# One running sum of the exponentials per attention unit, shared by VectorE and GpSimd

## The chip, the cores and the metric

The kernel runs on one core of a Trainium2 chip. The core has five engines with an instruction queue each: TensorE (PE, matmuls; its weight loads are shown apart as PEld), VectorE (DVE), ScalarE (ACT), GpSimd (POOL) and SyncE (SP), which only starts DMAs here. An engine takes its instructions strictly in the order of its queue; an instruction that waits holds everything behind it on the same engine. Engines are tied together by semaphores alone. The metric is the device time of one execution in microseconds.

## The reference

A trunk of two layers over 256 context and 1024 latent tokens of width 1024: a state-space mixer, then an attention mixer with 16 query heads and 4 key/value heads of 64, and a final norm. All is fp32. What matters here is the attention of the second layer, for the latent tokens only, with keys and values of all 1280 tokens:

```python
def attend(q, k, v):
    ...
    s = jnp.einsum('bqgrd,bkgd->bgrqk', q, k).astype(F32) * (A_HEADDIM ** -0.5)
    p = jax.nn.softmax(s, axis=-1).astype(v.dtype)
    o = jnp.einsum('bgrqk,bkgd->bqgrd', p, v)
...
o_lat = (ol * jax.nn.silu(gl)) @ out_w
...
h_lat = h_lat + gt[:, None] * o_lat
return rmsnorm(h_lat, final_norm_w)
```

## The kernel before

The first three quarters of the time go to the first layer and the projections of the second; the change leaves their instructions and order as they are. The attention and the output projection follow from 1475.6 us on.

**Units.** Attention is done in 16 units (`units`, `NU`): one unit is a pair of heads and 512 queries. A unit has ten key tiles of 128 keys (`kt`, `NT`). For each key tile, PE computes the scores of both heads into a PSUM buffer of 128 × 1024 (tag `sc`, three buffers; L1729, four matmuls a head: three for the split of fp32 into two parts, and one that subtracts the queries' maxima through a row of the query tile), ACT takes the exponential into an SBUF tile `P` of 128 × 1024 (L1734, six buffers), and PE multiplies it with the values into `ot` (L1745). The columns of `P` are queries, its partitions keys, so the softmax divisors are a sum over the ten tiles and then over the partitions. The first is done by adds of whole tiles into `acc` (L1710, L1754), the second by a matmul with ones (`divisors`, L1767, into PSUM tag `dn`).

**Divisors.** `keep` (L1771, ACT) copies `dn` into `rb`; `compact` (L1780) gathers one row of each head by DMA into `rv`, a 128 × 8 tile; DVE takes the reciprocals (L1787); two DMAs write them out (L1788) and spread them over the partitions again (L1784, into `rb`). Then `rb` is multiplied with the gate `sg` (L1790, POOL) and with the unit's output `ob` into `at` (L1791, DVE).

**Maxima.** The maxima of a unit's scores are computed ahead of it, from matmuls of their own with the queries as weights (`maxima`, L1528): ten tiles into `sc` buffers too, each reduced by DVE straight from PSUM (L1675), then one small reduction (L1543), a transpose on PE (L1684), a copy (L1687) and a DMA that puts them in the query tile (L1547). Units 0 and 1 have theirs from an earlier stage, so 14 units' maxima lie in this one.

**Rounds.** A unit is five rounds of two key tiles. In round r = 5u + j of unit u, PE's order is: first maxima tile of a later unit, scores of key tiles 2j and 2j + 1, second maxima tile, values of the round before. The maxima of unit u' are those of rounds 5u' − 8 to 5u' − 4. The divisors of unit u stand behind the values in round 5u + 6, the transpose of maxima at the end of a round whose number is 2 modulo 5. PE's order is given by numbers (`pe`, `turns`); the other engines' order comes from `Plan.order()`, a small planner that runs through the operations by rank, duration and dependencies, as written in each `plan.op`. What it gives is fixed in the program: the engines don't choose.

**PSUM.** With three `sc` buffers taken in turn by first maxima, two scores and second maxima, the second maxima of a round use the buffer that the first used, and can start only when DVE has reduced those.

**The two sums.** `SUM_POOL` gives key tiles 0, 1, 3, 5, 7 to POOL and the others to DVE. Each engine keeps a sum of its own (`acc` in two tags, one buffer each): POOL makes 0 + 1, then adds 3, 5, 7; DVE makes 2 + 4, then adds 6, 8, 9; a last DVE add (L1754) joins the two. POOL also does L1790 and, in eight units, the low part of a weight of the output projection (L1830, `wol`).

**Projection.** `project_out` runs over eight tiles of 128 tokens; the first four need only units 0 to 7. The high and low part of the first (`first`, L1857 and L1861) are made early, among the units. The rest stands behind the last unit.

Of the kernel before, what the change touches and what calls it, by code (L numbers as in the profile page):

```python
# [12 lines left out]
OP = mybir.AluOpType  # L13
# [16 lines left out]
SUM_POOL = (0, 1, 3, 5, 7)  # L30
WE = 4
SC_ACT, LO_POOL = (1, 4, 7), (1, 3, 5, 7)
# [113 lines left out]
def emit(tc, A, out):  # L146
# [1477 lines left out]
    with ExitStack() as st:  # L1624
# [10 lines left out]
        plan = Plan({"q": 3, "sc": 3, "ot": 1, "dn": 1, "P": NP, "accP": 1, "accV": 1, "mx": 2, "rb": 2, "sg": 2, "ob": 2, "wr": 4, "first": 2, "rv": 2})  # L1635
# [7 lines left out]
        held, shifts, brought, finished, last_scores, turns = {}, {}, {}, {}, [], []  # L1643

# [15 lines left out]
        def maxima(u):  # L1660
# [3 lines left out]
            for i in range(10):  # L1664
# [13 lines left out]
                rs.append(plan.op("DVE", reduce, [a], R + 10 * i - 60, 1.22, takes=[] if i else [hm], uses=[hs, hm]))  # L1678
            a = plan.op("DVE", lambda: largest(t["m"][1], t["m"][0]), rs, R + 30, .25, uses=[hm])
# [10 lines left out]
        def unit(u):  # L1690
# [3 lines left out]
            ho, hg, ha = plan.hold("ot"), plan.hold("sg"), {e: plan.hold("acc" + e[0] if e == "POOL" else "accV") for e in ("POOL", "DVE")}  # L1694
            sums = {"POOL": [], "DVE": []}
# [5 lines left out]
            def add_up(*tiles, e, rank):  # L1701

                if len(tiles) == 1:
                    return
                E, (k0, e0, h0), (kt, e1, h1), two = G if e == "POOL" else V, tiles[0], tiles[-1], len(tiles) == 2

                def add():
                    if two:
                        t[e] = S4.tile([128, 1024], FT, tag="acc" + e, bufs=1, name="acc")
                    E.tensor_tensor(t[e], t["P", k0] if two else t[e], t["P", kt], op=OP.add)  # L1710
# [5 lines left out]
            pv = None  # L1716
            for j in range(5):
# [31 lines left out]
                for i, kt in enumerate(kts):  # L1749
                    e = "POOL" if kt in SUM_POOL else "DVE"  # L1750
                    sums[e].append((kt, es[i], hp[i]))
                    add_up(*sums[e], e=e, rank=R + 10 * kt + 10)
            hd, hb, he = plan.hold("dn"), plan.hold("rb"), plan.hold("ob")
            a = plan.op("DVE", lambda: V.tensor_tensor(t["DVE"], t["DVE"], t["POOL"], op=OP.add), [t["aPOOL"], t["aDVE"]], R + 110, 1.3,  # L1754
                        uses=list(ha.values()))

# [7 lines left out]
            def divisors():  # L1764
                t["d"] = psum("dn", [128, 512])
                for h in range(2):
                    T.matmul(t["d"][h * 64:(h + 1) * 64], ones[:, 0:64], t["DVE"][:, h * 512:(h + 1) * 512], start=True, stop=True)  # L1767
# [5 lines left out]
            a = pe(5 * u + (6.6 if u < NU - 1 else 5.6), divisors, [a], R, .87, takes=[hd], uses=[ha["DVE"]], table="cols")  # L1773
# [8 lines left out]
            def spread():  # L1782
                for h, r in enumerate(HALF):
# [6 lines left out]
            a = plan.op("POOL", lambda: G.tensor_tensor(t["r"], t["r"], t["g"], op=OP.mult), [a, g], R + 90, 1.4, uses=[hb, hg])  # L1790
            finished[u] = plan.op("DVE", lambda: V.tensor_tensor(at[b][:, p], t["b"], t["r"], op=OP.mult), [a, ev], R + 90, .66,  # L1791
                                  uses=[hb, he])
# [43 lines left out]
        def table(i, src):  # L1836
            def bring():
                tabs[i] = S4.tile([128, 1024], FT, tag="acc" + ("POOL", "DVE")[i], bufs=1, name="tab")
                Q.dma_start(tabs[i], rows(src, 128))
# [144 lines left out]
```

## Time and profile before

| | us |
|---|---|
| runs shown: lowest, median, highest | 1970.56, 1971.6, 1972.78 |
| profiled execution: time, span of the core | 1970.99, 1969.2 |
| attention, first scores to the end of the last round with maxima | 1475.6 to 1829.1 |
| last two units and output projection on PE | 1829.1 to 1954.9 |
| after PE's last matmul | 1954.9 to 1969.2 |

Over the whole span PE is busy for 97%, DVE for 73%, ACT for 57%, POOL for 57%. These shares are averages over very different stages, so they are read by stretches here. A row of the timeline gives the start, the duration, the engine, the line of the kernel, what the instruction writes and reads, its shapes and a count; square brackets tell how long the engine stood idle before it and what released it. Matmuls overlap, so PE's busy time also holds small waits between them. The granted clock of PE is 1.00 all through the attention.

### The profile page before, as it was taken

How to read it: one execution, taken by the hardware profiler on the slowest of the kernel's cores; microseconds unless marked ns; L12 is line 12 of the kernel's file. 1: busy time of each engine (PE TensorE's matmuls, PEld its weight loads, DVE VectorE, ACT ScalarE, POOL GpSimd, SP SyncE). 2: the span in 40 equal slices, each digit the busy share in tenths (PEclk: the TensorE clock that was granted, in tenths of full speed). 3: DMA queues.
4: the chain of work that ended last, by engine and by line, in shares of the span. 5: the costliest groups of instructions: out<-in, count | busy, mean ns of one | idle time of the engine just before them, and what ended most of it. 6: DMA issues, size and time to landing. Idle time of an engine off the chain costs nothing.

```text
span 1969.2 us, 30433 instructions
## 1 busy us (share of the span) xinstructions
PE 1906.2 (97%) x10552; PEld 1448.0 (74%) x10552; DVE 1440.6 (73%) x1784; ACT 1115.2 (57%) x2055; POOL 1113.6 (57%) x940
## 2 busy tenths in 40 slices
PE   8999999999999999999999999999999999999997
PEld 2788788888888888888788878877774444444485
DVE  4677996979788786766446897877657888888533
ACT  4557767677867686777544775533224444444511
POOL 2305775668576766756388787753444444544422
PEclk9999999999999999999999999999999999999998
DMA  8125645444644546265585785533232111111123
GB/s 303 33 62 148 173 132 159 129 152 134 174 142 125 154 135 193 83 188 151 192 271 183 245 261 174 165 118 97 86 112 71 44 50 54 54 55 39 51 79 107
DMA packets 167614, 259.82 MB, mean 132 GB/s; under 512 B 24906, under 2 KB 60618, under 8 KB 167460
## 3 DMA queue, kind: packets, MB, share of 16 engines
q1 hardware_dynamic: 166308, 256.04, 42.7%
q8 instruction: 83, 1.36, 0.3%
q10 hardware_dynamic: 1152, 1.84, 0.2%
q14 instruction: 71, 0.58, 0.1%
HBM read 214.97 MB, written 42.69 MB: 131 GB/s over the span
## 4 chain that ended last, share of the span: by engine, by line
PE 69%; DVE 11%; POOL 2%; issue 2%; DMA 1%; ACT 1%; SPq 0%; DVEq 0%; POOLq 0%; ACTq 0%
PE ob L169 7%; PE pj L169 7%; PE pj L171 7%; PE ob L171 7%; PE pj L170 7%; PE ob L170 7%; PE ot L1745 6%; PE sc L1729 6%; PE yo L903 3%; DVE acc L1710 2%; PE sc L1528 2%; PE st L784 2%; DVE acc L711 2%; PE yd L861 2%; DVE mx L1675 1%
## 5 line engine op out<-in xcount | busy, mean ns | idle before, releaser
L169 PE MATMUL pj<-inh,whi 128*128 128x512 f32 (+1 forms) x1152 | 441.5, 383 | 0.5 <-DVE dv L519 0.5
L171 PE MATMUL pj<-inh,wlo 128*128 128x512 f32 (+1 forms) x1152 | 409.5, 355 | 1.2 <-POOL wlo L668 1.2
L170 PE MATMUL pj<-inl,whi 128*128 128x512 f32 (+1 forms) x1152 | 408.4, 355 | 0.0
L171 PEld LDWEIGHTS pj<-inh,wlo 128*128 128x128 f32 x1152 | 217.0, 188 | 33.3 <-POOL wlo L668 1.4
L711 DVE SCALAR_TENSOR_TENSOR acc<-ub,convw,acc 128x1282 f32<-128x1282 f32 x128 | 230.2, 1799 | 14.5 <-ACT acc L708 11.4
L169 PEld LDWEIGHTS pj<-inh,whi 128*128 128x128 f32 x1152 | 218.1, 189 | 28.5 <-issue 2.2
L1734 ACT ACTIVATE P<-sc 128x1024 f32<-128x1024 f32 x160 | 156.2, 1023 | 143.5 <-PE sc L1729 143.5
L170 PEld LDWEIGHTS pj<-inl,whi 128*128 128x128 f32 x1152 | 218.2, 189 | 25.5
L826 ACT ACTIVATE W<-lab,u_t 128x128 f32<-128x128 f32 x640 | 202.5, 391 | 50.0 <-POOL lab L820 24.4
L1675 DVE TENSOR_REDUCE mx<-sc 128x2 f32<-128x1024 f32 (+1 forms) x140 | 170.4, 1217 | 62.1 <-PE sc L1528 62.1
L820 POOL TENSOR_SCALAR_AFFINE_SELECT lab<-lab 128x512 f32<-128x512 f32 x160 | 146.7, 922 | 119.1 <-DMA lab<-la_d 110.0
L779 POOL TENSOR_TENSOR xw<-xst,te_t 128x256 f32<-128x256 f32 x144 | 147.4, 1039 | 23.7 <-PE st L784 12.0
L1745 PE MATMUL ot<-P,vv 128*64 128x512 f32 x640 | 155.0, 605 | 0.0
L1710 POOL TENSOR_TENSOR acc<-acc,P 128x1024 f32<-128x1024 f32 x48 | 115.5, 2406 | 54.9 <-ACT P L1734 53.7
L668 POOL TENSOR_TENSOR wlo<-wraw,whi 128x512 fp32r<-128x512 f32 x48 | 71.1, 1481 | 125.1 <-ACT whi L665 109.7
L1729 PE MATMUL sc<-q,kh 64*128 64x512 f32 x640 | 127.2, 393 | 0.2 <-ACT P L1734 0.2
L171 PE MATMUL ob<-whi,yl 128*128 128x512 f32 x288 | 113.9, 395 | 1.9 <-DVE yl L1127 1.3
L169 PE MATMUL ob<-whi,yh 128*128 128x512 f32 x288 | 114.6, 398 | 0.0
L170 PE MATMUL ob<-wlo,yh 128*128 128x512 f32 x288 | 113.7, 395 | 0.0
L968 DVE SCALAR_TENSOR_TENSOR macc<-mraw,cc,macc 128x512 f32<-128x512 f32 x98 | 107.8, 1122 | 2.9 <-DMA mraw<-in_mod_w 2.9
L798 POOL TENSOR_TENSOR tm<-PV,dec_t 128x512 f32<-128x512 f32 x64 | 89.5, 1398 | 35.2 <-DVE PV L802 33.6
L839 DVE TENSOR_TENSOR W<-W 128x512 f32<-128x512 f32 x80 | 73.9, 924 | 39.8 <-ACT W L826 38.6
(302 smaller groups left out, 4401.5 us busy)
## 6 DMA issues: line engine op xcount, KB each, us to landing
lab<-la_d SPq DMA_DIRECT2D x160, 256.0 KB
wraw<-in_w_in SPq DMA_DIRECT2D x96, 256.0 KB
workvv<-in_m_out_w SPq DMA_DIRECT2D x94, 256.0 KB
mraw<-in_mod_w SPq DMA_DIRECT2D x64, 256.0 KB
es<-e_d SPq DMA_DIRECT2D x128, 128.0 KB
wraw<-in_wqkv SPq DMA_DIRECT2D x48, 256.0 KB
q_d<-qs SPq DMA_DIRECT2D x64, 128.0 KB
q<-q_d SPq DMA_DIRECT2D x32, 256.0 KB
```

The lines of the kernel that those rows point to most:

```text
L169: T.matmul(o, lh, rh, start=first, stop=False)
L170: T.matmul(o, lh, rl, start=False, stop=False)
L171: T.matmul(o, ll, rh, start=False, stop=last)
L711: V.scalar_tensor_tensor(t["a"], ub[i % 2][:, k:k + CW], convw[:, ct, k:k + 1], t["a"], op0=OP.mult, op1=OP.add)
L779: G.tensor_tensor(t[d], s["xst"][:, c], te_t[:, d, c, h4][:, :, None].to_broadcast([128, 4, 64]), op=OP.mult)
L820: G.affine_select(t["l", d], t["l", d], [[0, 4], [sgn, 128]], OP.is_ge, NEVER, base=0, channel_multiplier=-sgn)
L826: S.activation(t["w", d][:, h], t["l", d][:, h], AF.Exp, bias=u_t[:, d, c, 4 * g + h:4 * g + h + 1])
L1675: V.tensor_reduce(max_place(t["m"][0], i), o, AX.X, OP.max)
L1710: E.tensor_tensor(t[e], t["P", k0] if two else t[e], t["P", kt], op=OP.add)
L1729: T.matmul(o[:, h], (first_row[r] if n == 3 else (kh, kl, kh)[n][r, kv, k]), x[(0, 0, 1, 2)[n]][r], start=(n == 0), stop=(n == 3))
L1734: S.activation(t["P", kt], flat(t["s", kt]), AF.Exp)
L1745: T.matmul(t["o"][h * 64:(h + 1) * 64], vv[:, kt, kv], t["P", kt][:, h * 512:(h + 1) * 512], start=(kt == 0), stop=(kt == NT - 1))
```

## The change

One sum per unit takes the place of two. DVE makes 0 + 1 and adds tiles 3, 5 and 7 (`SUM_DVE`); POOL adds tiles 2, 4, 6, 8 and 9 to the same `acc`. Each add waits for the one before it, so the two engines take turns, but for 8 and 9, which are both POOL's. There is no joining add. `acc` is one tag with two buffers, so the next unit's sum can begin before this one's is used.

The DVE adds get fixed places: `reduced[r]` is the reduction of the first maxima of round r, and `behind(r)` makes an operation wait for it in the plan. The first add of unit u stands behind that of round 5u + 1, tile kt's behind that of round 5u + 1 + kt // 2. The product with the gate moves from POOL to DVE, behind the first reduction of round 5u + 10, and so do the low parts of the early weights (one unit earlier than before). POOL's add of tile 9 waits for the product of the unit before (`finished[u - 1]` in the plan, and a dependency of the instruction itself on `scaled_by[u - 1]`). The two tables of the output projection use `acc`'s buffers as before, held as such.

```diff
-SUM_POOL = (0, 1, 3, 5, 7)
+SUM_DVE = (3, 5, 7)
...
-        plan = Plan({"q": 3, "sc": 3, "ot": 1, "dn": 1, "P": NP, "accP": 1, "accV": 1, "mx": 2, "rb": 2, "sg": 2, "ob": 2, "wr": 4, "first": 2, "rv": 2})
+        plan = Plan({"q": 3, "sc": 3, "ot": 1, "dn": 1, "P": NP, "acc": 2, "mx": 2, "rb": 2, "sg": 2, "ob": 2, "wr": 4, "first": 2, "rv": 2})
...
+        reduced, scaled_by = {}, {}
+
+        def behind(r):
+            return [reduced[r]] if r in reduced else []
...
+                if i % 2 == 0:
+                    reduced[5 * u - 8 + i // 2] = rs[-1]
...
-                t["a" + e] = plan.op(e, add, [e1, e0 if two else t["a" + e]], rank, 2.45 if e == "POOL" else 1.3,
-                                     takes=[ha[e]] if two else [], uses=[ha[e], h1] + ([h0] if two else []))
+            def add_first():
+                t["a"] = S4.tile([128, 1024], FT, tag="acc", bufs=2, name="acc")
+                V.tensor_tensor(t["a"], t["P", 0], t["P", 1], op=OP.add)
+
+            def add(kt):
+                x = (V if kt in SUM_DVE else G).tensor_tensor(t["a"], t["a"], t["P", kt], op=OP.add)
+                if kt == NT - 1 and u:
+                    tc.add_manual_dep(x.ins, scaled_by[u - 1].ins.name, mybir.DependencyInfo(mybir.DependencyClass.Sync, mybir.DependencyReason.DATA),
+                                      reason="sums")
+
+            def add_up():
+                last = plan.op("DVE", add_first, exps[0:2] + behind(5 * u + 1), R + 10, 1.25, takes=[ha], uses=[ha, *hps[0:2]])
+                for kt in range(2, NT):
+                    dve = kt in SUM_DVE
+                    last = plan.op("DVE" if dve else "POOL", lambda kt=kt: add(kt),
+                                   [last, exps[kt]] + (behind(5 * u + 1 + kt // 2) if dve else [finished[u - 1]] if kt == NT - 1 and u else []),
+                                   R + 10 * kt + 10, 1.25 if dve else 2.42, uses=[ha, hps[kt]])
+                return last
...
-            a = plan.op("DVE", lambda: V.tensor_tensor(t["DVE"], t["DVE"], t["POOL"], op=OP.add), [t["aPOOL"], t["aDVE"]], R + 110, 1.3,
-                        uses=list(ha.values()))
...
-            a = plan.op("POOL", lambda: G.tensor_tensor(t["r"], t["r"], t["g"], op=OP.mult), [a, g], R + 90, 1.4, uses=[hb, hg])
-            finished[u] = plan.op("DVE", lambda: V.tensor_tensor(at[b][:, p], t["b"], t["r"], op=OP.mult), [a, ev], R + 90, .66,
-                                  uses=[hb, he])
+            def scaled():
+                scaled_by[u] = V.tensor_tensor(at[b][:, p], t["b"], t["r"], op=OP.mult)
+
+            a = plan.op("DVE", lambda: V.tensor_tensor(t["r"], t["r"], t["g"], op=OP.mult), [a, g] + behind(5 * u + 10), R + 90, .66, uses=[hb, hg])
+            finished[u] = plan.op("DVE", scaled, [a, ev], R + 90, .66, uses=[hb, he])
...
-                R = 100 * (4 + 2 * kt + h) + 50 if kt < WE else 100 * NU + 10 * kt + 5 * h
+                R = 100 * (3 + 2 * kt + h) + 85 if kt < WE else 100 * NU + 10 * kt + 5 * h
...
-                after = last_scores if kt >= WE else [finished[3 + 2 * kt + h]]
+                after = last_scores if kt >= WE else [finished[2 + 2 * kt + h]]
+                early_slot = behind(5 * (5 + 2 * kt + h)) if kt < WE else []
...
-                wparts[kt, h] = plan.op("POOL" if kt < WE else "DVE", lambda t=t, f=part, E=G if kt < WE else V:
-                                        E.tensor_tensor(f(1), t["w"], f(0).bitcast(FT), op=OP.subtract), [a], R,
-                                        1.44 if kt < WE else .8, uses=[raw])
+                wparts[kt, h] = plan.op("DVE", lambda t=t, f=part: V.tensor_tensor(f(1), t["w"], f(0).bitcast(FT), op=OP.subtract), [a] + early_slot,
+                                        R, .7, uses=[raw])
```

DVE's queue of before, where unit 5's own sum begins (`acc_16466`, rounds 27 to 29; `mx` are reductions of maxima, `rv` the reciprocals of the unit before):

```order
L1675 TENSOR_REDUCE mx_16439<-sc_16424 128x2
L1675 TENSOR_REDUCE mx_16439<-sc_16456 128x2
L1710 TENSOR_TENSOR acc_16466<-P_16400,P_16454 128x1024
L1787 RECIPROCAL rv_16451<-rv_16451 128x8
L1675 TENSOR_REDUCE mx_16439<-sc_16471 128x2
L1675 TENSOR_REDUCE mx_16439<-sc_16500 128x2
L1710 TENSOR_TENSOR acc_16466<-acc_16466,P_16497 128x1024
L1675 TENSOR_REDUCE mx_16439<-sc_16512 128x2x2
L1675 TENSOR_REDUCE mx_16439<-sc_16542 128x2
L1710 TENSOR_TENSOR acc_16466<-acc_16466,P_16538 128x1024
L1675 TENSOR_REDUCE mx_16439<-sc_16553 128x2
L1710 TENSOR_TENSOR acc_16466<-acc_16466,P_16549 128x1024
```

The first two adds stand behind a round's second reduction, the later ones here and there; the joining add comes four rows further on.

DVE's queue of the changed kernel, rounds 25 to 27 (`acc_16401` is unit 5's sum; `rb` and `at` are unit 3's; the first row is the first reduction of round 25):

```order
L1680 TENSOR_REDUCE mx_16218<-sc_16332 128x2
L1838 TENSOR_TENSOR wol_15286<-wr_15316,woh_15285 128x512
L1799 TENSOR_TENSOR rb_16216<-rb_16216,sg_15937 128x512
L1797 TENSOR_TENSOR at0_15296<-ob_16170,rb_16216 128x512
L1680 TENSOR_REDUCE mx_16218<-sc_16357 128x2
L1680 TENSOR_REDUCE mx_16218<-sc_16373 128x2
L1709 TENSOR_TENSOR acc_16401<-P_16354,P_16367 128x1024
L1680 TENSOR_REDUCE mx_16218<-sc_16403 128x2x2
L1543 TENSOR_REDUCE nm0_10263<-mx_16218 128x8
L1680 TENSOR_REDUCE mx_16435<-sc_16421 128x2
L1712 TENSOR_TENSOR acc_16401<-acc_16401,P_16413 128x1024
L1680 TENSOR_REDUCE mx_16435<-sc_16453 128x2
```

Every add now stands between a round's first and second reduction; one round in five has the three products there instead.

POOL's queue of before, units 4 to 5 (`acc_16417` is POOL's sum of unit 5):

```order
L1790 TENSOR_TENSOR rb_16218<-rb_16218,sg_15932 128x512
L1830 TENSOR_TENSOR wol_15286<-wr_15316,woh_15285 128x512
L1710 TENSOR_TENSOR acc_16417<-P_16358,P_16370 128x1024
L1710 TENSOR_TENSOR acc_16417<-acc_16417,P_16415 128x1024
L1710 TENSOR_TENSOR acc_16417<-acc_16417,P_16463 128x1024
L1710 TENSOR_TENSOR acc_16417<-acc_16417,P_16507 128x1024
L1790 TENSOR_TENSOR rb_16436<-rb_16436,sg_16146 128x512
```

And POOL's queue of the changed kernel, the last add of unit 4 and those of unit 5:

```order
L1712 TENSOR_TENSOR acc_16184<-acc_16184,P_16328 128x1024
L1712 TENSOR_TENSOR acc_16401<-acc_16401,P_16399 128x1024
L1712 TENSOR_TENSOR acc_16401<-acc_16401,P_16450 128x1024
L1712 TENSOR_TENSOR acc_16401<-acc_16401,P_16492 128x1024
L1712 TENSOR_TENSOR acc_16401<-acc_16401,P_16533 128x1024
L1712 TENSOR_TENSOR acc_16401<-acc_16401,P_16545 128x1024
```

POOL has nothing but adds of the one sum, five a unit, each of tiles that DVE has handed on. PE's order is the same in both kernels up to the last unit; there the last divisors stand behind 24 matmuls of the projection's first tile, of which 12 stood behind them before.

More of the change, by code (lines that the diff above doesn't have):

```diff
@@ L1693, in unit @@
             x, q = qs3[u % 3], held[u]
-            ho, hg, ha = plan.hold("ot"), plan.hold("sg"), {e: plan.hold("acc" + e[0] if e == "POOL" else "accV") for e in ("POOL", "DVE")}
-            sums = {"POOL": [], "DVE": []}
+            ho, hg, ha = plan.hold("ot"), plan.hold("sg"), plan.hold("acc")
             def gate():
@@ L1837, in bring @@
             def bring():
-                tabs[i] = S4.tile([128, 1024], FT, tag="acc" + ("POOL", "DVE")[i], bufs=1, name="tab")
+                tabs[i] = S4.tile([128, 1024], FT, tag="acc", bufs=2, name="tab")
                 Q.dma_start(tabs[i], rows(src, 128))
-            return plan.op("SP", bring, [], 100 * NU + 200, takes=[plan.hold(("accP", "accV")[i])], move=1.75)
+            return plan.op("SP", bring, [], 100 * NU + 200, takes=[tab_holds[i]], move=1.75)
+        tab_holds = [plan.hold("acc") for _ in range(2)]
         in_tabs = [table(0, m_d[0, 3072:4096]), table(1, A["final_norm_w"])]
```

26 lines of the change are left out of this document (8 added, 18 removed).

## The prediction

> **What bounds the kernel now.** I read the busy time by stretches first, then the waits in the stretch that the change touches, then the chain that ended last there, then the timeline of one unit. The change leaves everything before 1475.6 us as it was, so only what follows counts. Stretches: length, then busy us of PE, PEld, DVE, ACT, POOL, granted clock, DMA share, GB/s.
>
> ```profile
> 1481.80:1829.10 347.30, 328.29 (x2089) 169.21 (x2087) 293.84 (x251) 161.34 (x189) 160.91 (x78) 1.00 0.16 48
> 1829.10:1954.90 125.80, 125.69 (x595) 88.34 (x593) 49.01 (x69) 39.56 (x63) 42.51 (x31) 1.00 0.25 80
> ```
>
> The first row is rounds 2 to 71 of attention, those with maxima of a later unit beside the scores. The second is the last two units (no maxima) and the output projection: PE is busy for 125.69 of 125.80 us, so nothing is to be had there. In the first, PE has 19.0 us without work and DVE is busy for 85%. Waits there (engine, line, who released it: total us, times, longest):
>
> ```profile
> PEld sc L1528 <- DVE mx L1675: 30.5, 29, 1.9
> PE sc L1528 <- DVE mx L1675: 18.9, 16, 1.5
> ```
>
> So PE waits, about twice in each of 14 units, for a reduction on DVE to free a PSUM buffer. What makes the reduction late shows in one unit on the timeline (start, us, engine, line, tiles, count, idle time before it):
>
> ```profile
> 1600.15 0.51 PE L1528 MATMUL sc<-kh,q 64*128 64x512 f32 x2
> ...
> 1605.41 0.50 PE L1528 MATMUL sc<-kh,q 64*128 64x512 f32 x2
> ...
> 1608.96 2.38 POOL L1710 TENSOR_TENSOR acc<-acc,P 128x1024 f32<-128x1024 f32 x1 [0.92 <-ACT P L1734]
> 1609.16 3.25 DVE L1710 TENSOR_TENSOR acc<-P 128x1024 f32<-128x1024 f32 x1
> ...
> 1610.00 0.50 PE L1528 MATMUL sc<-kh,q 64*128 64x512 f32 x2
> ...
> 1612.45 1.17 DVE L1675 TENSOR_REDUCE mx<-sc 128x2 f32<-128x1024 f32 x1
> ...
> 1613.67 0.50 PE L1528 MATMUL sc<-kh,q 64*128 64x512 f32 x2 [1.34 <-DVE mx L1675]
> 1613.93 2.36 POOL L1710 TENSOR_TENSOR acc<-acc,P 128x1024 f32<-128x1024 f32 x1 [2.59 <-ACT P L1734]
> ...
> 1615.36 2.01 DVE L1710 TENSOR_TENSOR acc<-acc,P 128x1024 f32<-128x1024 f32 x1
> ...
> 1615.97 0.50 PE L1528 MATMUL sc<-kh,q 64*128 64x256 f32 x4
> ...
> 1618.56 0.50 PE L1528 MATMUL sc<-kh,q 64*128 64x512 f32 x2 [0.23 <-DVE mx L1675]
> ...
> 1620.25 1.22 DVE L1710 TENSOR_TENSOR acc<-acc,P 128x1024 f32<-128x1024 f32 x1
> 1620.86 0.50 PE L1528 MATMUL sc<-kh,q 64*128 64x512 f32 x2
> ...
> 1621.41 1.23 DVE L1675 TENSOR_REDUCE mx<-sc 128x2 f32<-128x1024 f32 x1
> ...
> 1622.55 1.22 DVE L1710 TENSOR_TENSOR acc<-acc,P 128x1024 f32<-128x1024 f32 x1
> ...
> 1623.06 0.40 PE L1528 MATMUL sc<-kh,q 64*128 64x512 f32 x2
> ...
> 1623.68 0.69 DVE L1791 TENSOR_TENSOR at<-ob,rb 128x512 f32<-128x512 f32 x1
> ...
> 1624.28 1.22 DVE L1675 TENSOR_REDUCE mx<-sc 128x2 f32<-128x1024 f32 x1
> 1624.97 1.28 POOL L1830 TENSOR_TENSOR wol<-wr,woh 128x512 fp32r<-128x512 f32 x1 [6.10 <-ACT woh L1828]
> 1625.26 0.19 PEld L1528 LDWEIGHTS sc<-kh,q 64*128 64x128 f32 x2 [0.81 <-ACT woh L1828]
> ```
>
> The same add of 1024 columns takes 1.22 us at 1620.25 and 1622.55, with POOL silent, but 3.25 at 1609.16, where a POOL add had started 0.20 earlier. That POOL add ends at 1611.34, the DVE add at 1612.41, 1.07 later; the add of 2.01 us at 1615.36 ends 1.08 after its POOL neighbour (1613.93 + 2.36 = 1616.29). So a DVE add that meets a running POOL add stands until that is done and then runs. The reduction behind it starts at 1612.45, and PE, which in an undisturbed round issues its second maxima 2.20 us in (1620.86 to 1623.06), gets to them 3.67 us into the round that began at 1610.00. Rounds, from one first maxima matmul to the next: 1600.15 to 1605.41, 5.26 (with the divisors); to 1610.00, 4.59 (with the transpose); to 1615.97, **5.97**; to 1620.86, **4.89**; to 1625.26, 4.40. The last is a round without a wait. A unit of such rounds is 5.26 + 4.59 + 3 × 4.40 = **23.05 us**. What it takes now, from the chain that ended last (start, us, what), divisors of unit 0 and of unit 12:
>
> ```profile
> 1505.58 0.86 PE dn L1767 x4
> ...
> 1803.52 0.86 PE dn L1767 x4
> ...
> 1833.31 2.04 PE sc L1729 x16
> ...
> 1837.21 2.07 PE sc L1729 x16
> ```
>
> (1803.52 − 1505.58) / 12 = 24.83 us a unit: 1.78 us each are the stall.
>
> **The change, part by part.** *The adds.* Before, DVE has five adds a unit (first, three more, the merge) and POOL four, on two sums that run beside each other, hence collide. Now DVE has four and POOL five, on one sum: each add waits for the one before, so an add never runs beside another of its unit. On DVE an add stands right behind a round's first reduction. Its times in a round, counted from the round's first maxima matmul, come from the undisturbed round above (start 1620.86): first reduction at 1621.41, +0.55; the next DVE instruction at 1622.55, +1.69; with a 1.22 us add it is done at +2.91. The second maxima's reduction was late in that round (+3.42, behind an add and the product at L1791), and PE lost nothing by it. So one add in this gap costs nothing. For POOL's turn:
>
> ```profile
> 1601.84 1.21 DVE L1754 TENSOR_TENSOR acc<-acc 128x1024 f32<-128x1024 f32 x1
> ...
> 1603.20 2.36 POOL L1710 TENSOR_TENSOR acc<-P 128x1024 f32<-128x1024 f32 x1 [2.03 <-DVE acc L1754]
> ...
> 1622.43 1.94 ACT L1734 ACTIVATE P<-sc 128x1024 f32<-128x1024 f32 x2 [2.98 <-PE sc L1729]
> ```
>
> POOL took over 0.15 us after the DVE instruction that it waited for, so it starts at +3.06; its tile of exponentials (first of two, in 1622.43 to 1624.37) is done by about +2.6. With 2.38 us it ends at +5.44, that is +1.04 of the next round, 0.65 before DVE wants the sum back at +1.69. Round by round 1.22 + 0.15 + 2.38 = 3.75 us of a chain fit into 4.40. The collision goes, and no wait replaces it as long as that 0.65 holds. The reductions beside a running POOL add, and POOL's adds themselves:
>
> ```profile
> L1675 DVE TENSOR_REDUCE mx<-sc x140: 1167/1225/1228, 1482.4 to 1826.7; 128x2 f32<-128x1024 f32 x112, 128x4 f32<-128x1024 f32 x28
> ...
> L1710 POOL TENSOR_TENSOR acc<-acc,P x48: 2351/2380/3247, 1482.2 to 1857.1; 128x1024 f32<-128x1024 f32 x48
> ```
>
> (ns, shortest/median/longest.) None of 140 reductions took more than 1.228 us, with POOL adds beside many of them: reading PSUM, they don't meet POOL.
>
> The Trainium skill has a rule for this (SBUF — State Buffer, Who interferes with whom): a VectorE instruction with two SBUF inputs and a GpSimd instruction that reads SBUF exclude each other for the whole instruction, whichever starts first, while a tensor_reduce never contends. By that rule, the trace agrees (3.25 and 2.01 us against 1.22; reductions at most 1.228). The rule also speaks against this change at one place, since it puts two more such instructions of each unit on VectorE; that is the first rival below.
>
> *The products moved to DVE.* Per unit rb × sg (1.28 us on POOL at L1790, its row below) and, in eight units, the low part of a weight (1.28 on POOL at L1830, above) become DVE instructions of the L1791 size, 0.69 us, at a pitch of some 0.6. With L1791 they stand together behind the first reduction of one round: +1.69, +2.29, +2.89 to about 3.6; the second reduction ends at about 4.7; the next is wanted at 4.40 + 0.55 = 4.95. Nothing is lost. POOL's add of tile 8 is over at +1.04 of that round; its add of tile 9 is held until L1791 is done, so runs from about 3.75 to 6.13, that is +1.73 of the following round. The next unit's first add wants to start there at +1.69: 0.04 lost, hidden by the second reduction's slack. The divisors stand at the end of that round (+4.3), 2.6 later: no wait on PE.
>
> *What the products wait for.* They need a row of divisors that goes out and back by DMA:
>
> ```profile
> 1605.53 0.60 ACT L1771 ACTIVATE rb<-dn 128x512 f32<-128x512 f32 x1 [1.88 <-PE dn L1767]
> ...
> 1610.40 1.33 SPq L1547 DMA_DIRECT2D q<-mt  x2
> ...
> 1612.56 0.33 SPq L1788 DMA_DIRECT2D r_d<-rv  x1
> ...
> 1617.59 1.28 POOL L1790 TENSOR_TENSOR rb<-rb,sg 128x512 f32<-128x512 f32 x1 [1.30 <-DMA rb<-r_d]
> ...
> 1829.84 1.13 SPq L1780 DMA_DIRECT2D rv<-rb  x2
> ...
> 1833.73 0.20 DVE L1787 RECIPROCAL rv<-rv 128x8 f32<-128x8 f32 x1 [0.90 <-DMA rv<-rb]
> ```
>
> The copy at L1771 ends at 1606.13, +0.72 of its round; L1780 takes 3.89 to land (1829.84 to 1833.73), so the reciprocal, behind the round's second reduction (done near +4.05), stands until +4.6 and is over at +4.8, before the next reduction (4.59 + 0.55 = 5.14). Then L1788 to the product is 5.03 us (1612.56 to 1617.59). On SP it is issued behind the shift row (1610.40 to 1611.73, in a round that began at 1610.00), so at about +1.8 of the next round, so the row is there by +2.4 of the round after, and DVE asks for it 4.40 − 2.4 + 1.69 = 3.7 us later.
>
> *One low part of the projection.* `first`, 1024 columns, still stands among the rounds of unit 9:
>
> ```profile
> 1703.83 2.24 DVE first L1861
> ```
>
> It meets POOL's add, as it does now. Bounds 0 to 2.2 us, once; I take 0.3, because by the count above the reduction behind it comes some 0.3 after PE wants the buffer.
>
> *The tail.* With no maxima in the last two units, PE needs 3.90 us a round (scores at 1833.31 and 1837.21 above) and the chain 3.75, so the sum keeps up. The last divisors move behind 12 more projection matmuls (some 2.8 us), and POOL's last add is held by the unit before. PE has other work there; what could show is a weight part that comes late. Bounds −2 to +2 us; I take 0, since PE is busy for 125.69 of 125.80 us there now and its work is the same.
>
> **Sum.** Rounds 2 to 71 are 347.30 us now and 14 × 23.05 = 322.7 with no wait: −24.6; `first` +0.3; tail 0: **−24.3 us**. The profiled execution took 1970.99, so 1946.7; the median of the runs shown, 1971.6, is 0.6 above it, so **1947.3 us**. With the unknowns at their ends: 1945.0 to 1951.2.
>
> **Rivals.** *1. Part of the stall comes back.* If POOL's turns run later than counted by more than 0.65 us, DVE stands in front of the second reduction, and where three products stand together they are held by tile 8's add for up to 2.38 us. Then the second reduction ends at 2.38 later, 7.1, and the next round's first at 8.2, where PE wants it by 4.40 + 2.20 = 6.6: up to 1.6 us a unit, against 1.78 gained; in the middle 0.8, 14 × 0.8 = 11 us, so about **1958**. For it: the longest POOL add above is 3.247 us. Against it: the median is 2.380, and on one sum no add of the unit can meet another. *2. No change, 1971:* another wait in the round takes over in full. ACT is busy 161 of 347 us and no reduction is slowed, so I see no candidate; nor, since the queues' order is fixed, does the change fail to do what it says. *3. Slower.* The divisors' round trip now ends in DVE's queue, in front of reductions, instead of POOL's. Its slack is 3.7 us and the reduction has some 0.5 more (+1.69 against +2.20); from there each us costs PE one in each of 14 units. It outweighs the 1.78 gained when the trip is 6.0 us longer than in the rows; at 8 us longer it costs 14 × (8 − 6.0) = 28 us, so **2000**. DMA share is 0.16 here, so nothing suggests it.
>
> **Numbers.** Forecast 0.73 (1943 to 1951), first rival 0.15, no change 0.05, slower 0.07. A range of 1943 to 1959 leaves out the upper part of the first rival and the other two. A measurement can tell about 0.2% (3.9 us) from no change: faster 0.88, same 0.05, slower 0.07.
>
> **What would show it.** Right: divisors 23.05 us apart; DVE adds at 1.22 us with no group near 3; PE's waits for L1675's successor below 5 us in all; POOL waiting for DVE's sum in nearly every add. Wrong: DVE waiting for POOL before an add (rival 1) or for the DMA of rb (rival 3), or rounds of 4.40 us that have grown for a reason not listed.

## The result, and the profile after

| | before | after |
|---|---|---|
| median of 4 runs, us | 1971.87 (1970.56 to 1972.78) | **1947.09** (1945.63 to 1951.29) |
| ratio, 95% interval | | **0.9878** (0.9861 to 0.9895) |
| profiled execution: time, span | 1970.99, 1969.2 | 1945.63, 1943.9 |

The change is worth 24.8 us by the medians. The view of stretches, cut at the same two places of PE's order as before (first maxima of round 2; first scores of the last two units), says where they come from. Columns: length, then busy us of PE, PEld, DVE, ACT, POOL, granted clock, DMA share, GB/s; kernel after:

```profile
1482.89:1804.36 321.47, 321.32 (x2088) 169.27 (x2086) 256.84 (x258) 161.02 (x189) 167.66 (x71) 1.00 0.17 52
1804.36:1929.60 125.24, 125.24 (x594) 88.47 (x593) 52.71 (x69) 39.35 (x63) 42.64 (x30) 1.00 0.25 81
```

The rounds with maxima shrank from 347.30 to 321.47 us, by 25.83, and PE is now busy for 321.32 of 321.47: it had 19.0 us without work there and has 0.15. DVE's busy time fell by 37.0 us (293.84 to 256.84) although it now holds seven more instructions, since an instruction that stands and waits for POOL counts as busy. The stretch begins 1.09 us later than in the execution before (1482.89 against 1481.80), which lies ahead of anything the change touches, and what follows it on all engines is 0.56 us shorter (1969.2 − 1829.10 = 140.10, 1943.9 − 1804.36 = 139.54). −25.83 + 1.09 − 0.56 = −25.30 us is the difference of the two spans.

The waits of the same kernel from 1475 us on (engine, line, who released it: total us, times, longest):

```profile
POOL acc L1712 <- DVE acc L1712: 97.4, 42, 3.5
...
POOL acc L1712 <- DVE acc L1709: 39.7, 15, 17.3
POOL acc L1712 <- DVE at L1797: 35.5, 14, 2.8
...
DVE acc L1712 <- POOL acc L1712: 11.7, 7, 2.9
...
PEld sc L1528 <- DVE mx L1680: 0.6, 1, 0.6
...
PE sc L1528 <- DVE mx L1680: 0.2, 1, 0.2
```

PE's wait for the reduction that was 18.9 us in 16 places is 0.2 in one. POOL now waits for the other engine before 71 of its 80 adds; those waits are idle time of an engine that nobody waits for. DVE waits for POOL before an add seven times: once for 0.2 us at the start of the stretch, and six times in the last two units, where no maxima are left to delay.

One unit on the timeline (start, us, engine, line, operation, tiles, count, idle time before it): the round with three products, the round after it with the unit's first add, and the first add by each engine behind it.

```profile
1587.75 0.51 PE L1528 MATMUL sc<-kh,q 64*128 64x512 f32 x2
...
1588.30 1.23 DVE L1680 TENSOR_REDUCE mx<-sc 128x2 f32<-128x1024 f32 x1 [0.87 <-PE sc L1528]
...
1589.44 0.68 DVE L1838 TENSOR_TENSOR wol<-wr,woh 128x512 fp32r<-128x512 f32 x1
...
1590.04 0.69 DVE L1799 TENSOR_TENSOR rb<-rb,sg 128x512 f32<-128x512 f32 x1
...
1590.76 0.69 DVE L1797 TENSOR_TENSOR at<-ob,rb 128x512 f32<-128x512 f32 x1
...
1591.37 2.55 DVE L1680 TENSOR_REDUCE mx<-sc 128x2 f32<-128x1024 f32 x2
...
1591.62 2.39 POOL L1712 TENSOR_TENSOR acc<-acc,P 128x1024 f32<-128x1024 f32 x1 [2.82 <-DVE at L1797]
...
1592.15 0.50 PE L1528 MATMUL sc<-kh,q 64*128 64x512 f32 x2
...
1593.83 1.26 DVE L1709 TENSOR_TENSOR acc<-P 128x1024 f32<-128x1024 f32 x1
...
1597.39 0.50 PE L1528 MATMUL sc<-kh,q 64*128 64x512 f32 x2
...
1599.07 1.21 DVE L1712 TENSOR_TENSOR acc<-acc,P 128x1024 f32<-128x1024 f32 x1
...
1600.43 2.37 POOL L1712 TENSOR_TENSOR acc<-acc,P 128x1024 f32<-128x1024 f32 x1 [2.83 <-DVE acc L1712]
1601.34 0.19 DVE L1793 RECIPROCAL rv<-rv 128x8 f32<-128x8 f32 x1
...
1601.98 0.50 PE L1528 MATMUL sc<-kh,q 64*128 64x512 f32 x2
...
1606.33 0.51 PE L1528 MATMUL sc<-kh,q 64*128 64x256 f32 x4
...
1609.38 2.36 POOL L1712 TENSOR_TENSOR acc<-acc,P 128x1024 f32<-128x1024 f32 x1 [1.99 <-DVE acc L1712]
...
1610.70 0.50 PE L1528 MATMUL sc<-kh,q 64*128 64x512 f32 x2
```

Each add and product of DVE stands in the hole behind a first reduction, that is, in the time between it and the round's second, and POOL's add of tile 9 starts 0.17 us after the last product is done (1590.76 + 0.69, 1591.62). It runs beside reductions only, except at its end: it is over at 1594.01, 0.18 us into the next unit's first add, which lasts 1.26 us instead of 1.21. The five rounds, from first maxima to first maxima, are 4.40, 5.24, 4.59, 4.35 and 4.37: 22.95 us, with no round stretched. The chain that ended last gives the same period; divisors of unit 0 and of unit 13:

```profile
1504.81 0.86 PE dn L1773 x4
...
1803.57 0.86 PE dn L1773 x4
```

That is 13 periods of 22.95 us and 0.4 once, where `first` is made.

### The profile page after: what moved, and what is told of

Read it like the earlier page. It is cut to its first block, busy times and chain, and to the rows that moved or that the text cites. A ratio compares the mean times of both kernels' runs of the same rounds, so it can differ in the third digit from the quotient of the medians.

```text
span 1943.9 us, 30413 instructions
## 1 busy us (share of the span) xinstructions
PE 1898.8 (98%) x10552; PEld 1447.6 (74%) x10552; DVE 1409.8 (73%) x1792; ACT 1115.0 (57%) x2055; POOL 1117.3 (57%) x932
## 4 chain that ended last, share of the span: by engine, by line
PE 82%; DVE 7%; DMA 3%; POOL 3%; ACT 2%; issue 2%; SPq 0%; POOLq 0%; DVEq 0%; ACTq 0%
PE pj L169 9%; PE pj L171 9%; PE pj L170 9%; PE ot L1756 8%; PE sc L1740 7%; PE ob L169 7%; PE ob L171 7%; PE ob L170 7%; PE yo L903 3%; PE st L784 3%; DVE acc L711 2%; PE sc L1528 2%; PE yd L861 2%; PE tc L756 1%; PE sc L169 1%
## 5 line engine op out<-in xcount | busy, mean ns | idle before, releaser
L1712 POOL TENSOR_TENSOR acc<-acc,P 128x1024 f32<-128x1024 f32 x80 | 189.9, 2374 | 187.9 <-DVE acc L1712 97.4
L826 ACT ACTIVATE W<-lab,u_t 128x128 f32<-128x128 f32 x640 | 202.9, 391 | 48.6 <-POOL lab L820 24.3
```

The lines of the kernel that those rows point to most:

```text
L826: S.activation(t["w", d][:, h], t["l", d][:, h], AF.Exp, bias=u_t[:, d, c, 4 * g + h:4 * g + h + 1])
L1712: x = (V if kt in SUM_DVE else G).tensor_tensor(t["a"], t["a"], t["P", kt], op=OP.add)
```

## The experiments

A unit's period stands for the time: it is taken from the starts of the divisors' matmuls (`dn`) on PE.

| kernel | median us (lowest to highest) | ratio to before, 95% interval | unit, us |
|---|---|---|---|
| the changed kernel again | 1947.41 (1945.96 to 1948.08) | 0.9869 (0.9854 to 0.9884) | 22.95 |
| places alone, first try | 1972.27 (1970.89 to 1973.96) | 0.9997 (0.9987 to 1.0006) | 23.4 to 29.5 |
| places alone, PE's order kept | 1955.70 (1954.59 to 1957.16) | 0.9916 (0.9899 to 0.9932) | 23.70 |
| one sum, no places | 1967.87 (1964.77 to 1970.06) | 0.9974 (0.9962 to 0.9986) | 24.69 |
| one sum, places for the products only | 1980.61 (1978.69 to 1981.30) | 1.0040 (1.0025 to 1.0055) | 24.4, then 26.1 |
| without the hold on tile 9's add | 1954.63 (1953.71 to 1956.34) | 0.9908 (0.9893 to 0.9922) | 23.59, then 24.2 |
| product with the gate on POOL | 1950.05 (1943.85 to 1950.68) | 0.9877 (0.9860 to 0.9894) | 22.95 |
| one more POOL product | 1946.88 (1945.11 to 1947.54) | 0.9865 (0.9849 to 0.9882) | 22.95 |
| one more POOL memset | 1945.53 (1945.49 to 1948.25) | 0.9865 (0.9850 to 0.9879) | 22.95 |
| two more POOL memsets | 1946.15 (1945.92 to 1947.11) | 0.9868 (0.9853 to 0.9883) | 22.95 |

**The changed kernel again**, as the base of the others.

> The changed kernel once more, beside the runs it is compared with: 1945 to 1951 us, as in its four runs so far (median 1947.09).

It repeats: 0.9869.

**Places alone: two sums as before, DVE's adds put behind first reductions.** In the kernel before, with `reduced` and `behind` added as in the change:

```diff
-                t["a" + e] = plan.op(e, add, [e1, e0 if two else t["a" + e]], rank, 2.45 if e == "POOL" else 1.3,
+                t["a" + e] = plan.op(e, add, [e1, e0 if two else t["a" + e]] + (behind(5 * u + {4: 3, 6: 4, 8: 5, 9: 5}[kt]) if e == "DVE" else []), rank, 2.45 if e == "POOL" else 1.3,
...
-            a = plan.op("DVE", lambda: V.tensor_tensor(t["DVE"], t["DVE"], t["POOL"], op=OP.add), [t["aPOOL"], t["aDVE"]], R + 110, 1.3,
+            a = plan.op("DVE", lambda: V.tensor_tensor(t["DVE"], t["DVE"], t["POOL"], op=OP.add), [t["aPOOL"], t["aDVE"]] + behind(5 * u + 6), R + 110, 1.3,
```

> The kernel before, with its two sums, its joining add and the product with the gate on GpSimd, but VectorE's adds put behind a round's first reduction (first add behind that of round 5u+3, tile 6 of 5u+4, tiles 8 and 9 of 5u+5, the joining add of 5u+6). Theory A (the loss is VectorE adds that start while a GpSimd add runs and hold up the reduction behind them): GpSimd's adds of tiles 3, 5 and 7 start when the odd exponential is done, some 3.5 us into a round, and are over by about 1.5 of the next, VectorE's adds start at 1.69, so they hardly meet; rounds near 4.40, units 23 to 23.4 us, total 1947 to 1953. Theory B (one sum whose adds take turns is what brings it): the adds still meet, and the time stays at 1965 to 1972.

No gain: 0.9997, as theory B has it, but not for its reason. The adds of 3 us are gone (the longest is 2.26), but the edit was not the test it was meant to be. A wait in the plan says "not before", and the planner put tile 9's add behind the *second* reduction of its round. Timeline of that kernel, one such place:

```profile
1595.25 1.28 POOL L1836 TENSOR_TENSOR wol<-wr,woh 128x512 fp32r<-128x512 f32 x1 [4.43 <-ACT woh L1834]
...
1595.71 1.92 DVE L1716 TENSOR_TENSOR acc<-acc,P 128x1024 f32<-128x1024 f32 x1
...
1598.81 0.50 PE L1528 MATMUL sc<-kh,q 64*128 64x256 f32 x4 [0.92 <-DVE mx L1679]
```

There it met POOL's low part of a weight, and PE waited. In units 4 to 7 the period was 24.13 us; just before them, without a low part, it was 23.4 to 23.5. Later, 24 matmuls of the projection of `first` moved from the tail in among the rounds. That is some 5.5 us of work by the plan's 1.38 for six, yet the period from unit 9 to unit 13 became 27.7 us on average and stayed at 26.3 in rounds that got none of them. Their result holds one of the three `sc` buffers from the first of them on, and from 1700 us on PE also waits for reductions at the scores (8.0 us in 17 places, none before). So the total tells nothing of the places.

**Places alone, with PE's order kept.** As above, but the add of tile 9 and the join come early in the planner's ranks, so that tiles 8 and 9 stand together behind the first reduction, and the projection's matmuls are kept behind the last scores:

```diff
-                                     ... if e == "DVE" else []), rank, 2.45 if e == "POOL" else 1.3,
+                                     ... if e == "DVE" else []), rank - 160 * (kt > 7), 2.45 if e == "POOL" else 1.3,
...
-            ... + behind(5 * u + 6), R + 110, 1.3,
+            ... + behind(5 * u + 6), R - 150, 1.3,
...
-                mm = plan.op("PE", product, [mm, wparts[kt, 0], wparts[kt, 1]], R + kt, 1.38, takes=[] if kt else [hs], uses=[hs, hh, hl],
+                mm = plan.op("PE", product, [mm, wparts[kt, 0], wparts[kt, 1]] + last_scores, R + kt, 1.38, takes=[] if kt else [hs], uses=[hs, hh, hl],
```

> The kernel before with VectorE's adds at places, again, and this time with TensorE's order exactly that of before (the first projection tile waits for the last scores) and the adds of tiles 8 and 9 together behind the first reduction of round 5u+5, the joining add behind that of 5u+6. Two sums, joining add and product on GpSimd as before. Theory A (what costs is a VectorE add that meets a GpSimd add and so makes a reduction late): GpSimd's adds end at about 1.5 of a round, VectorE's start at 1.69 or later, so none is stretched; the round with two adds and the product ends its second reduction at 5.8 and costs about 0.3 us: units of 23.0 to 23.6 us, total 1948 to 1956. Theory B (two sums can't be had without the loss): units of 24.5 and more, total 1966 to 1973.

0.9916, inside theory A's range, with units 0.1 us above its 23.6: two sums with places take 1.08 us out of most units (24.78 to 23.70; the 24.83 of the prediction is a mean that holds two longer units). What is left to the changed kernel's 22.95, 0.75 us, shows in the round behind the one with two adds. Timeline of this kernel:

```profile
1638.24 0.51 PE L1528 MATMUL sc<-kh,q 64*128 64x512 f32 x2
...
1639.92 2.54 DVE L1716 TENSOR_TENSOR acc<-acc,P 128x1024 f32<-128x1024 f32 x2
...
1642.39 0.68 DVE L1797 TENSOR_TENSOR at<-ob,rb 128x512 f32<-128x512 f32 x1
1642.62 0.50 PE L1528 MATMUL sc<-kh,q 64*128 64x512 f32 x2
...
1642.99 2.35 DVE L1679 TENSOR_REDUCE mx<-sc 128x2 f32<-128x1024 f32 x2
...
1644.26 0.50 PE L1735 MATMUL sc<-q,kh 64*128 64x512 f32 x2 [0.22 <-DVE mx L1679]
...
1648.55 0.49 PE L1528 MATMUL sc<-kh,q 64*128 64x512 f32 x2
```

No instruction is stretched here; there is simply too much in one hole. Two adds (2.54 us together) and a product push the round's second reduction to 1642.99, 4.75 us after the round's first maxima. The next round's first reduction follows straight behind it, in the same row, so it is late too, PE waits, and that round lasts 5.93 us (1642.62 to 1648.55) instead of 5.24. Five DVE adds a unit did not find a place each here; the changed kernel's four do. Whether two sums could be had without this loss by other places was not tried.

**One sum, no places.** In the changed kernel `behind` returns nothing:

```diff
         def behind(r):
-            return [reduced[r]] if r in reduced else []
+            return []
```

> The changed kernel without the fixed places: one sum in turns, VectorE's adds and products where ranks and durations put them, mostly behind a round's second reduction. Theory A: adds of one unit can't meet, so most of the gain stays; where a product and an add stand together behind a second reduction, the next first reduction comes some 0.4 us late, and a weight part may meet an add: 14 units x 0.4 = 6 us, total 1949 to 1957. Theory C (the places bring it, the one sum doesn't): 1963 to 1972.

0.9974, in theory C's range, with units of 24.69 us: without the places, one sum in turns, with the products on DVE, is worth almost nothing. Timeline of this kernel:

```profile
1593.48 1.22 DVE L1680 TENSOR_REDUCE mx<-sc 128x2 f32<-128x1024 f32 x1
1593.71 2.37 POOL L1712 TENSOR_TENSOR acc<-acc,P 128x1024 f32<-128x1024 f32 x1 [1.99 <-DVE acc L1712]
...
1594.62 2.01 DVE L1799 TENSOR_TENSOR rb<-rb,sg 128x512 f32<-128x512 f32 x1
...
1596.66 0.69 DVE L1797 TENSOR_TENSOR at<-ob,rb 128x512 f32<-128x512 f32 x1
1597.27 1.22 DVE L1680 TENSOR_REDUCE mx<-sc 128x2 f32<-128x1024 f32 x1
...
1598.55 0.50 PE L1528 MATMUL sc<-kh,q 64*128 64x512 f32 x2 [1.15 <-DVE mx L1680]
```

No add meets another (none of DVE's takes more than 1.3 us), but the product with the gate, now on DVE, stands behind a second reduction and meets POOL's add of tile 8: 2.01 us instead of 0.69. The stall has changed its instruction, not its kind. What one sum without places would do with this product left on POOL was not run.

**One sum, places for the products only.** The two lines of `add_up` lose their `behind`; the projection's matmuls are kept behind the last scores as above:

```diff
-                last = plan.op("DVE", add_first, exps[0:2] + behind(5 * u + 1), R + 10, 1.25, takes=[ha], uses=[ha, *hps[0:2]])
+                last = plan.op("DVE", add_first, exps[0:2], R + 10, 1.25, takes=[ha], uses=[ha, *hps[0:2]])
...
-                                   [last, exps[kt]] + (behind(5 * u + 1 + kt // 2) if dve else [finished[u - 1]] if kt == NT - 1 and u else []),
+                                   [last, exps[kt]] + ([finished[u - 1]] if kt == NT - 1 and u else []),
```

> The changed kernel with places for the products on VectorE and with the hold of tile 9's add, but without places for the adds, so that the first add of a unit comes behind the second reduction of the round before its old place, right where GpSimd's last add of the unit before runs. Theory A, by count: that last add runs from 3.9 to 6.2 us of the round, the first add is held until 7.3, the next round's first reduction comes at 2.9 where it should at 0.55, and PE waits 1.5 to 2 us in each unit: units of 24.4 to 25, total 1964 to 1974. Theory D (one sum is enough once the products are out of the way): units of 23.0 to 23.4, total 1946 to 1953.

Slower than before, 1.0040, and above the range of theory A, whose mechanism it shows. Timeline of a unit with three products; the two rows of `values` show what came of it:

```profile
1595.87 1.94 PE L1756 MATMUL ot<-P,vv 128*64 128x512 f32 x8
...
1597.22 2.40 POOL L1712 TENSOR_TENSOR acc<-acc,P 128x1024 f32<-128x1024 f32 x1 [2.85 <-DVE at L1797]
...
1598.10 2.59 DVE L1709 TENSOR_TENSOR acc<-P 128x1024 f32<-128x1024 f32 x1
1600.62 1.21 DVE L1680 TENSOR_REDUCE mx<-sc 128x2 f32<-128x1024 f32 x1
...
1601.88 0.53 PE L1528 MATMUL sc<-kh,q 64*128 64x256 f32 x4 [1.81 <-DVE mx L1680]
...
1602.34 3.56 PE L1756 MATMUL ot<-P,vv 128*64 128x512 f32 x8
```

Now the next unit's first add, out of its place, meets POOL's add of tile 9, which the hold makes late; the first reduction behind it is late and PE stands for 1.81 us. In units 1 to 3, which have no low part of a weight, PE stands for 1.17 us and the period is 24.4. With a gap longer by 0.64 that makes 25.0 in the others; the rest of their period, some 26.1 us, is the granted clock. Stretches of the same kernel, columns as above:

```profile
1598.82:1602.23 3.41, 1.60 (x16) 1.00 (x12) 3.01 (x2) 1.94 (x2) 2.19 (x2) 1.00 0.02 5
1602.23:1605.65 3.42, 3.42 (x12) 1.00 (x10) 2.53 (x3) 0.00 (x0) 0.96 (x1) 0.50 0.00 0
```

After the gap the clock is 0.50 for 3.42 us, and eight matmuls of `values` take 3.56 us instead of 1.94. There are six such half-clock stretches from 1481 to 1830 us, and the clock there is 0.97 in the mean, where it was 1.00 before: 349 × 0.03 = 10 us. That is what the nine periods from the first of them to the last have over 25.0 us.

**Without the hold on tile 9's add.** In the changed kernel:

```diff
-                if kt == NT - 1 and u:
-                    tc.add_manual_dep(x.ins, scaled_by[u - 1].ins.name, ...)
...
-                                   [last, exps[kt]] + (behind(5 * u + 1 + kt // 2) if dve else [finished[u - 1]] if kt == NT - 1 and u else []),
+                                   [last, exps[kt]] + (behind(5 * u + 1 + kt // 2) if dve else []),
```

> The changed kernel without the wait of GpSimd's add of tile 9 for the product of the unit before. Theory A: that add starts right behind tile 8's, at about 1.0 us into the round with the three products, and runs to 3.4; the products wait for it, end at about 5.2, the second reduction at 6.4, the next round's first at 3.1, where PE wants it at 2.2: 0.9 us a unit, 13 us in all, total 1955 to 1962. Rival (a product that meets an add is hidden by the reductions' slack): 1945 to 1950.

0.9908, 7.2 us slower than the changed kernel run beside it: theory A's mechanism, with a total 0.4 us below its range. Groups of instructions between 1500 and 1830 us (count | busy us, mean ns), of this kernel:

```profile
L1796 DVE TENSOR_TENSOR rb<-rb,sg 128x512 f32<-128x512 f32 x14 | 19.3, 1381 | 1.2 <-DMA rb<-r_d 1.2
L1835 DVE TENSOR_TENSOR wol<-wr,woh 128x512 fp32r<-128x512 f32 x8 | 19.0, 2372 | 0.0
```

Whichever product comes first in its hole meets tile 9's add: the low part takes 2.37 us where there is one, the product with the gate some 2.3 in the six others ((19.3 − 8 × 0.68) / 6), instead of 0.69. Such an addition to the hole pushes the second reduction past its slack: units without a low part take 23.59 us, those with one 24.2.

**The product with the gate back on POOL.**

```diff
-            a = plan.op("DVE", lambda: V.tensor_tensor(t["r"], t["r"], t["g"], op=OP.mult), [a, g] + behind(5 * u + 10), R + 90, .66, uses=[hb, hg])
-            finished[u] = plan.op("DVE", scaled, [a, ev], R + 90, .66, uses=[hb, he])
+            a = plan.op("POOL", lambda: G.tensor_tensor(t["r"], t["r"], t["g"], op=OP.mult), [a, g], R + 90, 1.4, uses=[hb, hg])
+            finished[u] = plan.op("DVE", scaled, [a, ev] + behind(5 * u + 10), R + 90, .66, uses=[hb, he])
```

> The changed kernel with the product with the gate back on GpSimd (between the adds of tiles 8 and 9), the rest as in the change. By the count of theory A the product runs from about 1.0 to 2.3 us of the round, VectorE's last product follows behind the second reduction at about 3.6, tile 9's add runs until about 2.9 of the next round, and the next unit's first add, which wants to start at 1.69, is stretched to about 2.2 us. The second reduction's slack in that round (5.26 us long) takes that up: total 1945 to 1950, no loss. Rival (each meeting of a VectorE add with a GpSimd add costs PE what it costs the add): 14 x 1.0 = 14 us, 1958 to 1965.

0.9877, units of 22.95 us. So in the units the move of this product is worth nothing, though with the product on POOL a DVE add is held in every unit. Elsewhere the profiled execution loses: 0.9 us at `first` and 1.7 in the period of each of the last two units, of which 2.4 us remain from the first divisors to the end (441.7 against 439.3). The four runs scatter from 1943.85 to 1950.68, so the medians can't tell whether this is a cost. Group of instructions of this kernel between 1500 and 1830 us:

```profile
L1709 DVE TENSOR_TENSOR acc<-P 128x1024 f32<-128x1024 f32 x15 | 29.7, 1978 | 5.2 <-ACT P L1745 5.2
```

The unit's first add takes 1.98 us in the mean instead of 1.26, but behind a *first* reduction, where the second can be late.

**One more POOL instruction beside an add**, first a product that reads and writes, then a memset that only writes, then two of them. In the changed kernel, with `extra` and `extra2` as tiles of their own, cleared once:

```diff
                 x = (V if kt in SUM_DVE else G).tensor_tensor(t["a"], t["a"], t["P", kt], op=OP.add)
+                if kt == 4:
+                    G.tensor_tensor(extra, extra, extra, op=OP.mult)
```

> The changed kernel and one more GpSimd instruction in each unit, right behind its add of tile 4: a multiplication of a private 1024-column tile by itself, which nothing waits for. It runs from about 1.0 to 3.4 us of a round, across the place (1.69) of VectorE's add of tile 5. Theory A: that add takes about 2.8 us in place of 1.22; behind it the second reduction ends at 5.6 and the next first reduction at 2.3 of the next round, where PE wants it at 2.2: 0.1 to 0.3 us a unit, total 1947 to 1952. Theory of price by meeting (each such meeting costs PE its stretch): 14 x 1.6 = 22 us, 1967 to 1972.

> As the run before, but the extra GpSimd instruction is a memset of the same tile, which reads nothing. If what VectorE's add waits for is GpSimd's reading, tile 5's add keeps 1.22 us though GpSimd is busy beside it: total 1945 to 1950. If any GpSimd instruction holds it, the add is stretched to the end of the memset and about 1.07 us more. What a memset of 1024 columns takes no trace here shows.

> The changed kernel and two GpSimd memsets of 1024 columns behind the add of tile 4, since one took 0.95 us and ended as VectorE's add began. The two run from 1.0 to 2.9 us, across the add's start at 1.69. If only GpSimd's reading holds VectorE's add: the add keeps 1.22 us. If any GpSimd instruction does: 1.7 to 2.3 us. In either case no wait on PE, total 1944 to 1950.

The product takes 1.89 us, not the 2.4 that was counted, and makes a collision in every unit: DVE's next add takes 2.07 us and ends 1.09 us after POOL's product (1604.35 + 1.89 = 1606.24, 1605.26 + 2.07 = 1607.33), as the kernel before showed it. Yet units stay at 22.95 us and the time at 0.9865. Timeline of the kernel with the product:

```profile
1604.35 1.89 POOL L1715 TENSOR_TENSOR extra<-extra 128x1024 f32<-128x1024 f32 x1
...
1605.26 2.07 DVE L1713 TENSOR_TENSOR acc<-acc,P 128x1024 f32<-128x1024 f32 x1
```

One memset took only 0.95 us and was over as the add began, which tells nothing; two reach into the add. Timeline of the kernel with two:

```profile
1604.73 0.96 POOL L1717 MEMSET extra<- 128x1024 f32 x1
1604.76 1.22 DVE L1714 TENSOR_TENSOR acc<-acc,P 128x1024 f32<-128x1024 f32 x1
```

Beside a memset the add keeps its 1.22 us.

None of the kernels is faster than the changed one by more than the runs scatter.

## Why the prediction was right, point by point

- **The bound.** A late first reduction held PE: with it on time in every round, PE's idle time there is 0.15 us. The stall came out at 1.88 us a unit (24.83 − 22.95) against 1.78, since rounds of 5.24, 4.35 and 4.37 us exist where 5.26 and 4.40 were taken from one unit; that is 1.4 us of the total. PE's own waits, 18.9 us in 16 places, were about one a unit; the prediction's "about twice" counts those of the weight loads.
- **The turns.** POOL was to start 3.06 us into a round and does at 3.04 and 3.05 (1600.43, 1609.38); it was to end 1.04 into the next, and does (1609.38 + 2.36 against 1610.70). Neither is still running when DVE's next add or product starts, at 1.69 of the next round.
- **The products.** Starts at 1.69, 2.29 and 3.01 against 1.69, 2.29 and 2.89; tile 9's add ends at 1.86 of the next round against 1.73; the next first add is 0.05 longer against 0.04. No wait on PE, as said.
- **What they wait for.** The reciprocal was to stand until 4.6 us into its round. It starts at 3.95 (1601.34 − 1597.39), without a wait: the row came sooner than the 3.89 us of the one DMA in the last units that was taken for it. The step was wrong by 0.65 us and cost nothing, being in slack. The third rival (slower, by the round trip) had nothing to stand on: DVE waits for the DMA of `rb` twice, both times after 1804 us, where no maxima are left.
- **`first`** cost 0.4 us against 0.3, **the tail** −0.6 against 0. The sum was −24.3; the profiled executions differ by 25.3 and the medians by 24.8. That the total came so close is in part luck: the rounds gave 1.5 us more than −24.3 and the tail 0.6 more, and 1.1 us went ahead of the stretch, where the prediction has no term.
- **The first rival** (part comes back) did not happen, but its mechanism is real: without the hold, a product in that hole is stretched by 1.7 us (2.37 against 0.68; the rival says up to 2.38), by tile 9's add and not by tile 8's, and 0.6 to 1.3 us a unit come back.
- **What was missing.** "The collision goes" gives the one sum too much credit. One sum with the products on DVE but without places leaves 24.69 us a unit, the places with two sums 23.70, and tile 9's hold is worth 0.6 to 1.3. And a collision is not itself the price: put in again, in two kernels, behind a first reduction, it cost the units nothing. So the absence of adds near 3 us, named as a sign that it works, was not the sign that decides: the kernel with one sum and no places shows it too. PE's waits for the reductions, named beside it, were.

## What to carry to other kernels

An instruction that is held by another engine costs what the next instruction *that somebody waits for* loses: find in the in-order queue the hole with slack behind it (here behind the first of two reductions), and put everything that can be held there, but no more than fits: one add or three short products did, two adds and a product did not. Removing collisions by splitting the work otherwise only moves them to the next instruction that fits the pattern, as the kernel with one sum and no places shows. When a partial version of such a change comes out slower, look at the granted clock before counting waits.

## What the runs showed of the hardware

- **The clock after a short gap.** The kernel with places for the products only has eight gaps of 1.78 to 1.81 us without a matmul. Six of them were followed by 3.4 us at a clock of 0.50, two (1680.18 and 1731.90) were not, nor were the four shorter gaps of 1.17 to 1.46 us. The six half-clock stretches begin 27.3, 27.3, 51.2, 51.2 and 27.3 us after one another, that is 8, 8, 15, 15 and 8 times 3.41 us, as if on a fixed grid. Each of the six gaps lies wholly within the 3.41 us ahead of a half-clock stretch, so that PE is idle there for 1.78 to 1.81 us. Of the two others, one is cut by the grid (1.23 us on one side), and one begins 0.04 us ahead of it and leaves 1.74. Stretches of the latter, columns as above:

```profile
1731.94:1735.36 3.42, 1.68 (x10) 0.78 (x12) 2.82 (x3) 1.08 (x2) 2.35 (x1) 1.00 0.02 7
1735.36:1738.77 3.41, 3.41 (x24) 1.90 (x22) 2.62 (x4) 1.00 (x2) 0.00 (x0) 1.00 0.00 0
```

  The waits of up to 1.5 us in the kernel before were not followed by one either; its clock was 1.00 all through the attention. The Trainium skill (TensorE: Matmul & The Clock Gate, Why this matters for your kernels) asks for no idle gaps over some 3 us. By that rule these gaps should have been free; here the measurement decides, and 1.8 us were enough in six of eight. The eight cases fit a limit on PE's idle share of a fixed 3.41 us, between 1.74 and 1.78 us, and not one on the gap's length alone; this was read from one execution, and no run tested it.
- **Writes don't hold DVE.** A two-input add beside a memset of GpSimd took 1.22 us, beside a product 2.07. The Trainium skill (SBUF — State Buffer, Who interferes with whom) has it so: only a GpSimd instruction that reads SBUF contends with the second input. The trace agrees.
- **Dependent adds.** In the kernel with places alone and PE's order kept, two DVE adds of 1024 columns, the second on the first's result, stood 0.10 us apart in 13 of 14 units, so started 1.32 us apart where the first was not held; once, at 1617.55, the wait was 0.45 us, and why stays open. In the changed kernel a reduction, which doesn't use the add ahead of it, started 1.13 us after that add (1599.07, 1600.20).
